# A decoder block with product-key experts: rows of the expert sum moved between POOL and DVE, one engine for a weighting, and one form for all V tiles

## The chip, the core and the metric

One core of a Trainium2 chip. The metric is device time in microseconds (us) of one execution. Engines are named as in the profile: PE (TensorE), DVE (VectorE), ACT (ScalarE), POOL (GpSimd), SP (SyncE, which here only issues DMAs).

## What is computed

A decoder block on 512 tokens of width 1024: three attention branches, merged by gates and added to x, then a sum over experts that are looked up for each token. Only the second part is touched here:

```python
v1, i1 = lax.top_k(s1, 16)                  # per head (8): scores against 128 keys, twice
v2, i2 = lax.top_k(s2, 16)
sv, si = lax.top_k(v1[..., :, None] + v2[..., None, :], 16)
experts = e1 * 128 + e2                     # 128 experts per token out of 16384
act = gelu(h . u[experts]) * softmax(sv)
x = x + sum(act * v[experts])
```

u and v are tables of 16384 rows of 1024 float32 numbers.

## The kernel before

The 512 tokens are four blocks of 128. Blocks 0 and 1 go the sparse way, blocks 2 and 3 the dense way.

**Sparse: rows.** For each of a block's 128 slots, POOL issues an indirect DMA (line 832) that fetches one row of u for each of the 128 tokens, 128 x 1024 numbers; DVE multiplies it by h and sums (line 842), into acts. After 128 such u rows come 128 v rows, which DVE adds to x1 with their weights (line 851, `step`). The 512 rows stand in one list, JOBS, and `step` takes the next. There is a second form for v rows, `apart=True`: ACT scales the row (line 847) and POOL adds it to x1 (line 848). Rows are fetched ahead into buffers, 4 in general, 6 where `ahead` is AHEAD + MORE, so that with the one in use up to seven are under way. All v rows of a block add into the same tile (mg in the profile), one after the other.

**Dense.** For blocks 2 and 3 PE multiplies h by all of u, in 128 tiles of 128 experts (`dense_u`, line 953: 8 float32 matmuls of 256 columns, which the profile records as 16), and ACT's gelu writes the activations (ga, line 955). The gates are spread from the chosen slots over all experts ("spreading", below). Then PE multiplies the 128 activation tiles by all of v (`dense_v`, the V stage).

**The stages at the end, in program order.** (1) The search for blocks 1 to 3: scores on PE, top 16 on DVE (MAX, MATCH_REPLACE, MAX_INDEX), candidates on POOL (line 688). A credit lets one v row of block 0 in for every PER_ROW = 2.8 units of search, in the form on POOL. (2) From here on the order on POOL, DVE and PE is that of the program. PE does 24 u tiles (COVER); DVE does `weigh`, then the choices of blocks 2, 3 and 1 (`choose`, lines 771 to 801: which candidates were chosen, by small integer steps and comparisons in bf16) and turns block 1's into row numbers (`numbers_of`, lines 811 to 815). Then come 12 more v rows (BETWEEN). (3) Spreading: 64 batches of 4 tokens. DVE compares slot numbers with 0..127 (line 1008, tile o), the result is weighted by the gates (three batches of four on ACT, line 1014, the fourth on POOL, line 1011), PE multiplies (line 1026), DVE multiplies the kept part into ga (line 1029), ACT copies the rest out (line 1032). A batch is built three ahead of its use. Each batch brings 0.7 rows (STEPS_N), and 25 u tiles are laid between the matmuls. (4) The V stage, 128 steps k. `operands(k+1)`: a V tile is fetched three ahead; three of four are split, hi on ACT (line 1075, whi) and lo on DVE (line 127, wlo), as are the activations (ah line 1073, al line 1077); from k = 32 on ga is first multiplied by its gates (line 1068). PE then does 12 matmuls (lines 141 to 143). Each fourth tile (k % WHOLE == 3) is taken whole, from a buffer of its own (last), in float32 with 4 matmuls, recorded as 8 (line 1091). The 71 u tiles that remain are spread over the first 118 steps, the rows that remain over the first 123.

DVE, PE, POOL and ACT each take their instructions strictly in order.

Of the kernel before, what the change touches and what calls it, by code (L numbers as in the profile page):

```python
# [12 lines left out]
AF = mybir.ActivationFunctionType  # L13
OP = mybir.AluOpType
# [7 lines left out]
NK = 128  # L22
# [4 lines left out]
DENSE = (2, 3)  # L27
# [2 lines left out]
FIRST_U, COVER, DURING, AFTER = 8, 24, 25, 0  # L30
KEPT = FIRST_U + COVER
SPILT = (128 - KEPT) // 2
BETWEEN, UNWEIGHED, IN_RAW = 12, 14, 0
LAG = FIRST_U + COVER + DURING + AFTER
GA_LATE = 6
URING = 6
# [2 lines left out]
GQ_AT, GQ_PARTS = 1, 4  # L39
RAW_MORE = 5  # L40
STEPS_U = 4
WHOLE, STEPS_N = 4, 0.7
AHD = 3
GSPLIT = 4
GT = 4
# [3 lines left out]
AHEAD, ROWS_IN, MORE = 4, 5, 2  # L49
LATER = 400  # L50
PACE = {"search": 9.0, "choose": 8.0, "rows": 3.5}
EARLY_ROWS, PER_ROW = 176, 2.8


@with_exitstack
def tile_block(ctx: ExitStack, tc: tile.TileContext, t: dict, out: bass.AP):
# [947 lines left out]
    def build_sides(n):  # L1004
        i, _, ts = tokens(n)
        eT = slots[i]
        o = sp.tile([128, 2, GT, NK], F32, tag="o", name="o", bufs=AHD + 1)
        V.tensor_tensor(o, numbers[:, None, None, :].to_broadcast([128, 2, GT, NK]),
                        eT[:, :2, ts, None].to_broadcast([128, 2, GT, NK]), op=OP.is_equal)
        if n % 4 == 3:  # L1010
            G.tensor_tensor(o[:, 0], o[:, 0], eT[:, 2, ts, None].to_broadcast([128, GT, NK]), op=OP.mult)
        else:
            for u in range(GT):
                A.activation(o[:, 0, u], o[:, 0, u], AF.Copy, scale=eT[:, 2, ts.start + u:ts.start + u + 1])
# [35 lines left out]

    def fetch_v(k):
        if k < NK:
            pool, n = (gp[0], 1) if k % WHOLE == WHOLE - 1 else (wp, None)
            tag = "last" if n else "raw"
            raw = pool.tile([128, D if n else WSLOT], F32, tag=tag, name=tag, **({"bufs": n} if n else {}))
            v_raw[k] = raw[:, :D]
            nc.sync.dma_start(v_raw[k], t["peer_v"][k * NK:(k + 1) * NK])

    def operands(k):

        whole = k % WHOLE == WHOLE - 1
        fetch_v(k + VFAR)
        get_gates(k + GK, k % GK - GQ_AT)
        raw, a = v_raw.pop(k), ga(k)
        if k >= KEPT:
            m = gq[k - k % GK][:, :, k % GK]
            g = a.rearrange("p (g t) -> p g t", t=TG)
            V.tensor_mul(g, m, g)  # L1068
        if whole:
            return whole, [raw], a, a  # L1070
        ah = gp[0].tile([128, TD], F32R, tag="ah", name="ah")
        al = gp[0].tile([128, TD], F32R, tag="al", name="al")
        A.copy(ah, a)  # L1073
        hi = wp.tile([128, WSLOT], F32R, tag="whi", name="whi")[:, :D]
        A.copy(hi, raw)  # L1075
        w = [x[:, 0] for x in rest((raw, hi, 1, 1), 0.0)]
        V.tensor_sub(al, a, ah.bitcast(F32))
        return whole, w, ah, al

    def dense_v(k, whole, w, ah, al):  # L1080
        if k == 0:
            tags = ["tp", "tp", "sc", "sc"]
            for i in range(ND):
# [2 lines left out]
        for i in range(ND):  # L1086
            tok = slice(i * 128, i * 128 + 128)
            for hf in range(2):
                d = slice(hf * 512, hf * 512 + 512)
                if whole:  # L1090
                    PE.matmul(acc[i, hf], al[:, tok], w[0][:, d], start=k == 0, stop=k == NK - 1)
# [19 lines left out]
    late.append(lp.tile([128, GA_LATE, TD], F32, name="late"))
# [143 lines left out]
```

## Time and profile before

| | us |
|---|---|
| three runs | 1653.95, 1659.4, 1661.33 |
| median | 1659.4 |
| the profiled execution | 1664.65 |
| its span, first to last instruction | 1662.9 |
| mean granted clock of PE | 0.983 |
| POOL's adds of v rows (line 848) | 34, 81.6 busy |
| POOL's weightings (line 1011) | 16, 27.4 busy |
| split V tiles (casts, line 1075) | 96 |

The span is 1.75 us shorter than the time of its execution. Busy times of matmuls overlap, since matmuls are pipelined; where the length of a group of them matters, it is read from the start of one group to the start of the next. In a row of the timeline, the first number is the start, the second the busy time, both in us; the bracket at the end is idle time before the instruction, with what ended it.

### The profile page before, as it was taken

The numbers are of one execution on the slowest core, as the hardware profiler recorded it, in microseconds if no ns is written. First come the engines' busy times: TensorE is split into PE (matmuls) and PEld (weight loads), VectorE is DVE, ScalarE is ACT, GpSimd is POOL, SyncE is SP. The second block draws the span as 40 slices with busy tenths as digits, with TensorE's granted clock in tenths as the row PEclk, the third lists the DMA queues.
The fourth block names the chain that finished last, engine by engine and source line by source line (L and its number), as shares of the span: only waits on it lengthen the run. The fifth ranks groups of instructions, "written<-read, shape, count | busy, mean of one in ns | idle before, by whom it ended". The sixth has DMA issues, their size and how long they took to land.

```text
span 1662.9 us, 25044 instructions
## 1 busy us (share of the span) xinstructions
PE 1579.9 (95%) x8622; PEld 1359.9 (82%) x8622; DVE 1346.5 (81%) x2599; ACT 700.0 (42%) x1562; POOL 806.9 (49%) x656
## 2 busy tenths in 40 slices
PE   5999999999998989997989999999999999999998
PEld 5999799888987988986878998677777777777775
DVE  5677358898988999998989998677777778778886
ACT  6787347545344434544316664222222222222221
POOL 1100012766565555689944545454554455455542
PEclk9999999999998999999999999999999999999999
DMA  7586744998998899867878999999999999999995
GB/s 291 187 277 220 253 143 144 318 345 306 344 314 301 294 334 349 275 216 274 279 274 298 341 352 354 398 409 378 361 392 400 401 388 402 401 401 398 402 366 214
DMA packets 178479, 531.77 MB, mean 320 GB/s; under 512 B 17584, under 2 KB 46512, under 8 KB 178352
## 3 DMA queue, kind: packets, MB, share of 16 engines
q0 software_dynamic: 73728, 268.47, 43.6%
q1 hardware_dynamic: 100016, 249.11, 41.4%
q10 hardware_dynamic: 4608, 12.58, 2.0%
q8 instruction: 68, 1.11, 0.3%
q14 instruction: 59, 0.48, 0.1%
HBM read 515.42 MB, written 14.68 MB: 319 GB/s over the span
## 4 chain that ended last, share of the span: by engine, by line
PE 36%; issue 20%; DMA 20%; POOL 12%; DVE 9%; ACT 2%; SPq 0%; POOLq 0%; DVEq 0%; ACTq 0%
DMA row<-in_peer_v_dram,eidx 10%; POOL row L832 9%; PE mm L953 8%; DMA row<-in_peer_u_dram,eidx 8%; PE mm L142 5%; PE mm L141 5%; PE mm L143 5%; POOL mg L848 2%; PE mm L294 2%; DVE mg L851 2%; PE sc L1026 2%; PE tp L1026 2%; DVE wlo L127 2%; DVE scr L842 1%; PE sc L493 1%
## 5 line engine op out<-in xcount | busy, mean ns | idle before, releaser
L832 POOL DMA_INDIRECT row<-in_peer_u_dram,eidx x256 | 320.2, 1251 | 254.4 <-DVE scr L842 193.7
L832 POOL DMA_INDIRECT row<-in_peer_v_dram,eidx x256 | 319.5, 1248 | 247.5 <-DVE mg L851 170.4
L127 DVE TENSOR_TENSOR wlo<-raw,whi 128x1024 fp32r<-128x1024 f32 (+1 forms) x243 | 307.3, 1266 | 60.0 <-ACT whi L115 33.0
L842 DVE SCALAR_TENSOR_TENSOR scr<-row,own 128x1024 bf16<-128x1024 f32 x256 | 313.6, 1225 | 43.7 <-DMA row<-in_peer_u_dram,eidx 38.5
L851 DVE SCALAR_TENSOR_TENSOR mg<-row,acts,mg 128x1024 f32<-128x1024 f32 x222 | 284.6, 1282 | 44.1 <-DMA row<-in_peer_v_dram,eidx 39.9
L953 PE MATMUL mm<-h2f,hhi 128*128 128x256 f32 x960 | 223.1, 383 | 3.3 <-ACT ga L955 3.2
L953 PE MATMUL mm<-h2f,hlo 128*128 128x256 f32 x960 | 219.6, 379 | 0.9 <-ACT ga L955 0.9
L953 PEld LDWEIGHTS mm<-h2f,hlo 128*128 128x128 f32 x960 | 179.9, 190 | 33.5 <-issue 8.1
L953 PEld LDWEIGHTS mm<-h2f,hhi 128*128 128x128 f32 x960 | 181.3, 192 | 29.3 <-ACT ga L955 4.5
L115 ACT CAST whi<-raw 128x1024 fp32r<-128x1024 f32 (+1 forms) x148 | 154.9, 1049 | 93.0 <-PE mm L142 45.7
L1075 ACT CAST whi<-raw 128x1024 fp32r<-128x1024 f32 x96 | 100.2, 1045 | 140.6 <-DMA raw<-in_peer_v_dram 136.3
L188 POOL TENSOR_TENSOR rsy<-rsv,mhalf 128x4 f32<-128x4 f32 (+5 forms) x25 | 38.8, 1553 | 221.4 <-DVE rsv L187 127.5
L955 ACT ACTIVATE ga<-mm 128x256 f32<-128x256 f32 x116 | 44.1, 382 | 235.2 <-PE mm L953 225.2
L141 PE MATMUL mm<-hhi,whi 128*128 128x384 f32 x320 | 110.3, 345 | 6.5 <-ACT ga L955 5.3
L142 PE MATMUL mm<-hlo,whi 128*128 128x384 f32 x320 | 110.6, 346 | 0.0
L143 PE MATMUL mm<-hhi,wlo 128*128 128x384 f32 x320 | 109.8, 343 | 0.0
L141 PE MATMUL mm<-whi,hhi 128*128 128x256 f32 (+1 forms) x360 | 104.6, 292 | 3.0 <-DVE g L571 1.9
L142 PE MATMUL mm<-wlo,hhi 128*128 128x256 f32 (+1 forms) x360 | 103.1, 287 | 0.5 <-DVE wlo L127 0.5
L143 PE MATMUL mm<-whi,hlo 128*128 128x256 f32 (+1 forms) x360 | 101.7, 284 | 0.0
L141 PE MATMUL sc<-whi,ah 128*128 128x512 f32 x192 | 90.8, 473 | 3.6 <-ACT ah L1073 2.9
L848 POOL TENSOR_TENSOR mg<-mg,row 128x1024 f32<-128x1024 f32 x34 | 81.6, 2399 | 0.7
L1073 ACT CAST ah<-ga 128x256 fp32r<-128x256 f32 x87 | 34.9, 404 | 107.7 <-DVE ga L1068 69.1
(281 smaller groups left out, 3479.8 us busy)
## 6 DMA issues: line engine op xcount, KB each, us to landing
raw<-in_peer_v_dram SPq DMA_DIRECT2D x96, 512.0 KB
hlo<-in_uT_dram SPq DMA_DIRECT2D x60, 512.0 KB
hhi<-in_uT_dram SPq DMA_DIRECT2D x60, 512.0 KB
raw<-in_w_tr_dram SPq DMA_DIRECT2D x48, 512.0 KB
raw<-in_w_nat_dram SPq DMA_DIRECT2D x40, 512.0 KB
last<-in_peer_v_dram SPq DMA_DIRECT2D x32, 512.0 KB
raw<-in_w_o_dram SPq DMA_DIRECT2D x24, 512.0 KB
gd<-st ACTq DMA_DIRECT2D x32, 384.0 KB
```

What stands on the lines that cost most here:

```text
L115: A.copy(hi[:, :n * w], raw[:, :n * w])
L127: V.tensor_sub(lo, raw, hi.bitcast(F32))
L141: PE.matmul(ps, lh, rh, start=first, stop=False)
L142: PE.matmul(ps, lh, rl, start=False, stop=False)
L143: PE.matmul(ps, ll, rh, start=False, stop=last)
L832: G.indirect_dma_start(out=r, out_offset=None, in_=t["peer_" + tab], in_offset=bass.IndirectOffsetOnAxis(ap=eidx[b][:, j:j + 1], axis=0))
L842: V.scalar_tensor_tensor(scr, r, 1.0, h2n[b], op0=OP.mult, op1=OP.mult, accum_out=acts[b][:, c]))
L848: G.tensor_tensor(x1[b], x1[b], r, op=OP.add)
L851: V.scalar_tensor_tensor(x1[b], r, acts[b][:, c], x1[b], op0=OP.mult, op1=OP.add))
L953: PE.matmul(ps[:, :TD], w[:, dc], h2f[dc], start=dc == 0, stop=dc == KC - 1)
L1026: PE.matmul(ps[:, u], o[:, 1, u], o[:, 0, u], start=True, stop=True)
L1075: A.copy(hi, raw)
```

## The change

**Fewer rows on POOL, rows among the choices.** PER_ROW goes from 2.8 to 4.6. By the order of instructions POOL adds 19 v rows instead of 34. The 12 rows behind the choices go; instead a row is let in for each unit that the choices spend (AMONG = 1.0), which gives 36, on DVE. On POOL, at the end of the search, before (mg is the sum, cand the candidates, row a fetched row):

```order
L848 TENSOR_TENSOR mg_2246<-mg_2246,row 128x1024
L688 TENSOR_TENSOR cand<-v_8832 128x3x8
L688 TENSOR_TENSOR cand<-v_8832 128x3x16
L832 DMA row<-in_peer_v_dram,eidx_176 128x1024
L848 TENSOR_TENSOR mg_2246<-mg_2246,row 128x1024
L832 DMA row<-in_peer_v_dram,eidx_176 128x1024
L848 TENSOR_TENSOR mg_2246<-mg_2246,row 128x1024
```

After, at the same place:

```order
L848 TENSOR_TENSOR mg_2246<-mg_2246,row 128x1024
L688 TENSOR_TENSOR cand<-v_8780 128x3x8
L688 TENSOR_TENSOR cand<-v_8780 128x3x16
L832 DMA row<-in_peer_v_dram,eidx_176 128x1024
L848 TENSOR_TENSOR mg_2246<-mg_2246,row 128x1024
L832 DMA row<-in_peer_v_dram,eidx_176 128x1024 x57
L832 DMA row<-in_peer_u_dram,eidx_178 128x1024 x128
```

Up to here the two are alike; before, 15 more pairs of fetch and add follow (the last two rows shown are the first pair), after it only the fetches of rows that DVE will add.

On DVE, in the first choice, before (rj, rb, hot: steps of the choice):

```order
L784 TENSOR_TENSOR rj<-rj,p_9253 128x128
L785 TENSOR_TENSOR rj<-p_9254,rj 128x128
L789 CAST rb<-ri 128x128
L791 CAST idb<-ids_7514 128x128
L794 TENSOR_TENSOR hot<-rb,iota_k 128x2048
L797 TENSOR_TENSOR hot<-hot,idb 128x2048
L800 TENSOR_TENSOR hot<-hot 128x1024
L800 TENSOR_TENSOR hot<-hot 128x512
L800 TENSOR_TENSOR hot<-hot 128x256
```

After, at the same place:

```order
L784 TENSOR_TENSOR rj<-rj,p_9193 128x128
L785 TENSOR_TENSOR rj<-p_9194,rj 128x128
L851 SCALAR_TENSOR_TENSOR mg_2246<-row,acts_177,mg_2246 128x1024
L789 CAST rb<-ri 128x128
L791 CAST idb<-ids_7514 128x128
L794 TENSOR_TENSOR hot<-rb,iota_k 128x2048
L851 SCALAR_TENSOR_TENSOR mg_2246<-row,acts_177,mg_2246 128x1024
L797 TENSOR_TENSOR hot<-hot,idb 128x2048
L851 SCALAR_TENSOR_TENSOR mg_2246<-row,acts_177,mg_2246 128x1024 x2
L800 TENSOR_TENSOR hot<-hot 128x1024
L800 TENSOR_TENSOR hot<-hot 128x512
L800 TENSOR_TENSOR hot<-hot 128x256
```

Rows (L851) now stand among the choice's steps, one or two at a time.

**Spreading.** All 64 weightings are on ACT. STEPS_N goes from 0.7 to 0.8: 51 rows in place of 44.

**V stage.** No tile is whole; each fourth one still has its own buffer (last) but is split like the others. 230 rows are left for it in place of 246. DVE at the beginning of the V stage, before (wlo and al are the lo halves, scr a u row):

```order
L127 TENSOR_TENSOR wlo<-raw,whi 128x1024
L1077 TENSOR_TENSOR al<-ga,ah 128x256
L842 SCALAR_TENSOR_TENSOR scr,acts_179<-row,own 128x1024 x4
L127 TENSOR_TENSOR wlo<-raw,whi 128x1024
L1077 TENSOR_TENSOR al<-ga,ah 128x256
L842 SCALAR_TENSOR_TENSOR scr,acts_179<-row,own 128x1024 x2
```

After:

```order
L127 TENSOR_TENSOR wlo<-raw,whi 128x1024
L1071 TENSOR_TENSOR al<-ga,ah 128x256
L842 SCALAR_TENSOR_TENSOR scr,acts_179<-row,own 128x1024 x2
L127 TENSOR_TENSOR wlo<-last,whi 128x1024
L1071 TENSOR_TENSOR al<-ga,ah 128x256
L842 SCALAR_TENSOR_TENSOR scr,acts_179<-row,own 128x1024 x2
```

The tile from the buffer last, which DVE did not touch before, now has its own wlo and al, and fewer rows stand between two tiles.

The diff, without the lines that only drop the flag `whole`:

```diff
-BETWEEN, UNWEIGHED, IN_RAW = 12, 14, 0
+AMONG, UNWEIGHED = 1.0, 14
-WHOLE, STEPS_N = 4, 0.7
+SPARE, STEPS_N = 4, 0.8
-EARLY_ROWS, PER_ROW = 176, 2.8
+EARLY_ROWS, PER_ROW = 176, 4.6
...
-        if n % 4 == 3:
-            G.tensor_tensor(o[:, 0], o[:, 0], eT[:, 2, ts, None].to_broadcast([128, GT, NK]), op=OP.mult)
-        else:
-            for u in range(GT):
-                A.activation(o[:, 0, u], o[:, 0, u], AF.Copy, scale=eT[:, 2, ts.start + u:ts.start + u + 1])
+        for u in range(GT):
+            A.activation(o[:, 0, u], o[:, 0, u], AF.Copy, scale=eT[:, 2, ts.start + u:ts.start + u + 1])
...
-        if whole:
-            return whole, [raw], a, a
...
-                if whole:
-                    PE.matmul(acc[i, hf], al[:, tok], w[0][:, d], start=k == 0, stop=k == NK - 1)
-                else:
-                    mm3(acc[i, hf], (ah[:, tok], al[:, tok]), (w[0][:, d], w[1][:, d]), k == 0, k == NK - 1)
+                mm3(acc[i, hf], (ah[:, tok], al[:, tok]), (w[0][:, d], w[1][:, d]), k == 0, k == NK - 1)
...
-    for lb in (1, 2):
-        list(choose(cp, f, lb, iota_k, chosen[DENSE[lb - 1]]))
-    list(numbers_of(cp, f, 0, 1, iota_k))
+    ahead[0] = AHEAD + MORE
+    credit[0] = 0.0
+    for job in (*(choose(cp, f, lb, iota_k, chosen[DENSE[lb - 1]]) for lb in (1, 2)), numbers_of(cp, f, 0, 1, iota_k)):
+        for cost in job:
+            credit[0] += cost
+            while credit[0] >= AMONG and done[0] < known[0]:
+                credit[0] -= AMONG
+                step()
     known[0] = len(JOBS)
-    ahead[0] = AHEAD + MORE
-    for _ in range(BETWEEN):
-        step()
```

More of the change, by code (lines that the diff above doesn't have):

```diff
@@ L1052, in fetch_v @@
         if k < NK:
-            pool, n = (gp[0], 1) if k % WHOLE == WHOLE - 1 else (wp, None)
+            pool, n = (gp[0], 1) if k % SPARE == SPARE - 1 else (wp, None)
             tag = "last" if n else "raw"
@@ L1059, in operands @@
     def operands(k):
-        whole = k % WHOLE == WHOLE - 1
         fetch_v(k + VFAR)
@@ L1077, in operands, with dense_v @@
         V.tensor_sub(al, a, ah.bitcast(F32))
-        return whole, w, ah, al
-    def dense_v(k, whole, w, ah, al):
+        return w, ah, al
+    def dense_v(k, w, ah, al):
         if k == 0:
```

## The prediction

> **What bounds the kernel now.** I read the page first, then busy time by stage, then the timeline of each engine where one stage meets the next.
>
> ```profile
> PE 1579.9 (95%) x8622; PEld 1359.9 (82%) x8622; DVE 1346.5 (81%) x2599; ACT 700.0 (42%) x1562; POOL 806.9 (49%) x656
> ```
>
> The shares are averages, so I cut the end of the run into its stages. Columns: stretch, length, then busy us (instructions) of PE, weight loads, DVE, ACT, POOL, the granted clock, the DMA share and GB/s.
>
> ```profile
> 774.30:820.40 46.10, 42.00 (x181) 34.74 (x179) 42.91 (x37) 21.38 (x30) 42.60 (x25) 0.96 0.82 274
> 820.40:865.60 45.20, 45.17 (x210) 39.75 (x211) 42.68 (x65) 4.86 (x13) 20.99 (x15) 1.00 0.72 249
> 865.60:876.00 10.40, 0.47 (x4) 0.26 (x3) 6.97 (x6) 1.46 (x5) 6.55 (x5) 0.73 1.03 416
> 876.00:1022.50 146.50, 146.50 (x917) 135.70 (x918) 137.94 (x180) 101.46 (x345) 70.16 (x59) 0.98 0.92 332
> 1022.50:1622.50 600.00, 594.98 (x2437) 460.16 (x2436) 457.42 (x625) 149.35 (x253) 307.12 (x236) 1.00 1.02 391
> 1622.50:1662.90 40.40, 32.52 (x109) 20.86 (x107) 26.29 (x34) 7.68 (x11) 8.30 (x6) 0.95 0.58 212
> ```
>
> The first two rows are the three choices on DVE, with the 24 covering u tiles on PE. The third is a hole: PE does 0.47 us in 10.4. The fourth is the spreading, where PE never stops and DVE nearly never. The fifth is the V stage while u tiles last: PE 595 of 600 us, so it is PE that sets its length, with DVE at 76% and the DMA engines full. The sixth is its tail, which no single engine fills. The chain that ended last shows the hole again:
>
> ```profile
> 865.92 9.93 issue
> 875.85 2.05 PE sc L1026 x8
> ```
>
> PE has ended the covering tiles at 865.9 and starts the spreading at 875.85, since the one-hot sides it needs come late from DVE. DVE's timeline, and POOL's adds of rows, tell why:
>
> ```profile
> 779.30 2.90 DVE L771 TENSOR_SCALAR sh<-pos 128x128 uint32<-128x128 uint32 x1
> 817.37 3.12 DVE L773 TENSOR_SCALAR sh<-pos 128x128 uint32<-128x128 uint32 x1
> 840.12 0.22 DVE L771 TENSOR_SCALAR sh<-pos 128x128 uint32<-128x128 uint32 x1
> 840.63 0.23 DVE L773 TENSOR_SCALAR sh<-pos 128x128 uint32<-128x128 uint32 x1
> 852.31 0.29 DVE L811 SCALAR_TENSOR_TENSOR e<-e,e 128x128 f32<-128x128 f32 x1
> 853.97 10.52 DVE L851 SCALAR_TENSOR_TENSOR mg<-row,acts,mg 128x1024 f32<-128x1024 f32 x8
> 874.10 4.61 DVE L1008 TENSOR_TENSOR o<-tg,eT 128x1024 f32<-128x1024 f32 x4
> ```
>
> ```profile
> 772.45 2.36 POOL L848 TENSOR_TENSOR mg<-mg,row 128x1024 f32<-128x1024 f32 x1
> 776.07 2.38 POOL L848 TENSOR_TENSOR mg<-mg,row 128x1024 f32<-128x1024 f32 x1
> 829.03 2.35 POOL L848 TENSOR_TENSOR mg<-mg,row 128x1024 f32<-128x1024 f32 x1
> ```
>
> The same small shift takes 0.23 us alone and 3.12 us while POOL adds a row: DVE stands still for the add. The third choice runs undisturbed, 840.12 to 852.31: 12.2 us. Three of them and the last three steps of the numbers (852.31 to 853.97) make 38.2 us; they took 74.7 (779.30 to 853.97). So POOL's late adds cost DVE 36 us, and the 12 rows behind them 20 us more (853.97 to 874.10).
>
> **Part 1: fewer rows to POOL, rows among the choices.** By the order POOL keeps 19 of its 34 adds, 36 rows stand among the choices in place of 12 behind them. The nineteenth add is the one at 772.45 (829.03 is the last, 15 follow the nineteenth), over at 774.8, before the choices begin at 779.3. So the 36 us of stalls go. What comes in is 24 more rows on DVE, and a row's price stands in the spreading, in three batches of DVE's timeline:
>
> ```profile
> 926.51 1.28 DVE L851 SCALAR_TENSOR_TENSOR mg<-row,acts,mg 128x1024 f32<-128x1024 f32 x1
> 927.70 0.28 DVE L1029 TENSOR_TENSOR ga<-tp,ga 128x128 f32<-128x128 f32 x1
> 930.22 0.28 DVE L1029 TENSOR_TENSOR ga<-sc,ga 128x128 f32<-128x128 f32 x1
> 931.56 0.28 DVE L1029 TENSOR_TENSOR ga<-tp,ga 128x128 f32<-128x128 f32 x1
> ```
>
> A row between other work costs 1.19 us (926.51 to 927.70), one behind another 1.32 (the 10.52 / 8 above); the order has mostly singles, so 1.25: 36 x 1.25 = 45 us. DVE would end at 779.3 + 38.2 + 45 = 862.5, against 874.1, and PE could start 1.75 us later, as now (874.10 to 875.85): 864.3. Is PE there? Its cover:
>
> ```profile
> 781.48 8.86 PE L953 MATMUL mm<-h2f,hhi 128*128 128x256 f32 x32 [2.74 <-ACT ga L955]
> 834.35 10.52 PE L953 MATMUL mm<-h2f,hlo 128*128 128x256 f32 x48
> 844.71 10.52 PE L953 MATMUL mm<-h2f,hhi 128*128 128x256 f32 x48
> 775.12 3.62 PE L953 MATMUL mm<-h2f,hhi 128*128 128x256 f32 x16
> ```
>
> Three u tiles take 10.36 us (834.35 to 844.71), one 3.45, 24 from 775.12 on 82.9; with the 2.74 us wait kept and 0.3 for transposes PE ends at 861. So the hole closes to about 3 us and the spreading starts 11.6 us earlier. The rows must come in time: POOL issues them, with nothing else to do, and up to seven are under way. Of today's twelve the last four came late; the first and the last of these, with the wait in brackets:
>
> ```profile
> 866.55 1.28 DVE L851 SCALAR_TENSOR_TENSOR mg<-row,acts,mg 128x1024 f32<-128x1024 f32 x1 [2.05 <-issue]
> 872.90 1.28 DVE L851 SCALAR_TENSOR_TENSOR mg<-row,acts,mg 128x1024 f32<-128x1024 f32 x1 [0.45 <-DMA row<-in_peer_v_dram,eidx]
> ```
>
> These waits are 0.45 to 2.05 us, behind eight rows taken back to back. The new ones stand 2.3 us apart (82 us for 36), so I charge 2.6 us in all. Behind a DVE that waits for a row stands the rest of the choices, and PE waits for that. **Term: -9 us** (0 to -11.6).
>
> **Part 2: spreading, 51 rows in place of 44, all weighting on ACT.** By the rows L1029 above a batch with a row takes DVE 2.52 us (927.70 to 930.22), one without 1.34. Seven rows more are 8.3 us: 137.9 + 8.3 = 146.2 of today's 146.5. PE was full, so nothing is gained; DVE is now as full as PE, and its 8.6 us of waits can't all be used. Between 0 (all used) and +8.3 (none) I take **+3.5 us**. ACT gets 16 x 4 more weightings:
>
> ```profile
> L1014 ACT ACTIVATE o<-o,eT 128x128 f32<-128x128 f32 x191 | 60.8, 390 | 17.0 <-DVE o L1008 13.7 <-issue 3.3
> ```
>
> 64 x 60.8/191 = 20.4 us, so 122 busy of 146.5. Three batches of lead cover that; if not, rival D. On POOL the weightings stood ahead of the rows' issues; without them rows come no later, for which I take nothing.
>
> **Part 3: every V tile split.** 16 rows leave the V stage (246 to 230), and 32 whole tiles become split ones.
>
> ```profile
> 1404.10 1.88 PE L1091 MATMUL sc<-last,ga 128*128 128x512 f32 x4
> 1407.53 3.62 PE L953 MATMUL mm<-h2f,hlo 128*128 128x256 f32 x16
> 1410.80 0.58 PE L141 MATMUL sc<-whi,ah 128*128 128x512 f32 x1
> 1413.76 0.39 PE L141 MATMUL sc<-whi,ah 128*128 128x512 f32 x1
> 1416.51 3.62 PE L953 MATMUL mm<-h2f,hlo 128*128 128x256 f32 x16
> ```
>
> Their busy times overlap, so I read from start to start. A whole tile: 1404.10 to 1407.53, 3.43 us. A split one: 1413.76 to 1416.51, 2.75 us, or 2.96 behind a u tile, which is then itself 3.27 in place of 3.45. Either way a split tile saves about 0.66 us of PE. The Trainium skill, "FP8 and Floating Point Precision", TensorE Precision Notes, says that true FP32 makes four passes through the array; three reduced passes would then be 3/4 of 3.43, 0.86 us saved, and this term an estimated 25 us where the rows give 19. While u tiles last (118 of 128 tiles, 29 of them whole) that is 29 x 0.66 = 19 us. In the tail PE isn't the bound, and I take nothing. The cover of this term is DVE:
>
> ```profile
> L851 DVE SCALAR_TENSOR_TENSOR mg<-row,acts,mg 128x1024 f32<-128x1024 f32 x119 | 152.7, 1283 | 33.6 <-DMA row<-in_peer_v_dram,eidx 32.3
> L842 DVE SCALAR_TENSOR_TENSOR scr<-row,own 128x1024 bf16<-128x1024 f32 x118 | 144.3, 1223 | 26.1 <-DMA row<-in_peer_u_dram,eidx 22.0 <-issue 1.3 <-DVE scr L842 0.9
> L127 DVE TENSOR_TENSOR wlo<-raw,whi 128x1024 fp32r<-128x1024 f32 x90 | 111.0, 1234 | 26.4 <-ACT whi L1075 20.6 <-issue 3.9 <-ACT ga L955 1.9
> L1077 DVE TENSOR_TENSOR al<-ga,ah 128x256 fp32r<-128x256 f32 x81 | 34.0, 420 | 48.4 <-ACT ah L1073 47.7 <-ACT whi L1075 0.6
> ```
>
> Each split tile adds a 1.234 us and a 0.420 us subtraction: 29 x 1.654 = 48 us; 16 rows at 1.25 take away 20. DVE goes from 457 to 485 us of a stage of 581: 84% for 76%. ACT, at 149 of 600, has room for two more casts a tile. On SP the buffer of every fourth tile comes free when DVE has split it, no longer when PE is done with it, so its load is issued no later. The DMA engines are full too, but 16 rows of 0.524 MB (128 x 1024 x 4 bytes) are 8.4 MB less, at 391 GB/s 21 us: were they the bound, the gain would be the same. With some waits on the fuller DVE: **-17.5 us** (-21 to -9, rival A's end).
>
> **Sum.** -9 + 3.5 - 17.5 = -23 us on the profiled execution's 1664.65: 1641.65. That execution lies 5.25 above the median of the runs shown, 1659.4; on that scale 1636.4.
>
> **The rivals.** *A, DVE paces the V stage.* Its idle time in rows L127 and L1077 (75 us) is waiting for ACT's halves, which may come with every tile: with 32/24 of it, 485 + 100 = 585, more or less, and with some of the row waits 591. The stage gains 9 us, the sum is -14.5: 1644.9. *B, the same with nothing given up:* if all 142.6 us of idle time (600 - 457.4) stay, the stage takes 628, and the sum is +22.5: 1681.9. Against B: 60 us of that idle time are rows that DVE came too early for, and a later DVE doesn't wait for them. *C, slower: the rows among the choices come late.* The place is POOL's issue:
>
> ```profile
> L832 POOL DMA_INDIRECT row<-in_peer_v_dram,eidx x256: 935/993/3086, 562.1 to 1632.1; - x128
> ```
>
> An issue takes 0.99 us in the middle and 3.09 at worst (min/median/max). If each of the 36 takes the worst and 0.3 between, DVE ends at 780.6 + 36 x 3.39 = 903, the spreading starts 28.5 us late, and the sum is +14.5: 1673.9. It decides from 3.0 us a row on, where the start is 14 us late and the sum is nothing; below 2.3 it costs nothing. The median speaks against it. The Trainium skill, "SBUF — State Buffer", SBUF: two separate sides, says that POOL can't write a DMA's descriptors while certain DVE operations hold the shared port; by that rule C's stretched issues would be the common case among the choices, but the median above says that they are rare in the whole run. *D, ACT paces the spreading:* should all its 45 us of waits stay beside 122 of work, the stage takes 167, 20.4 more, and the sum is -6.1: 1653.3.
>
> **How the numbers follow.** The forecast gets 0.57, A 0.17, B 0.06, C 0.10, D 0.10. A measurement of this kernel can tell about 0.5%, 8.3 us, from no change. Forecast and A are faster; D and a third of C's way lie within; B and the rest of C are slower: 0.74, 0.13, 0.13. The low end takes every best bound: -11.6 + 0 - 21 = -32.6, 1626.8, and 2 us for the scatter of the runs: 1625. The high end takes in D and C up to where the sum is nothing, and 2.6 for the scatter: 1662. Left out are about 0.13 above and 0.05 below.
>
> **What would show it.** Right: no DVE shift over 1 us behind the search; spreading starting near 865 with a hole of PE under 5 us; 148 to 152 us of spreading; the V stage with PE still near 99% and some 582 us to the last u tile. Wrong: rows among the choices with waits that sum to over 15 us (C), PE waiting for wlo or al in the V stage (A, B), ACT full and PE waiting for it in the spreading (D).

## The result and the profile after

The kernel after takes 1633.94 us (median of 4 runs, 1632.55 to 1638.87) against 1660.37 for the kernel before on the same chip (4 runs): the ratio is 0.9853, with a 95% interval from 0.9819 to 0.9888. A ratio is always the time of the kernel named over that of the kernel before, with its 95% interval in brackets. A second measurement with the experiments gave 0.9846 (0.982 to 0.9872). The profiled execution of after took 1635.28 us (span 1633.5), 29.4 less than that of before (1664.65, span 1662.9). Busy time and the shares of the chain that ended last, on the page of after:

```profile
PE 1559.2 (95%) x8750; PEld 1384.0 (85%) x8750; DVE 1368.6 (84%) x2678; ACT 743.4 (46%) x1675; POOL 788.7 (48%) x625
PE 68%; DMA 11%; DVE 7%; issue 7%; POOL 3%; ACT 2%; SPq 0%; DVEq 0%; POOLq 0%; ACTq 0%
```

PE stood for 36% of that chain before; POOL fell from 12% to 3% and "issue" from 20% to 7%. For a comparison by stage both traces are cut at the same events: the first u tile of the cover, the first matmul of the spreading, the end of the spreading, the last u tile, the end. Busy time by stage (columns as in the prediction), of before and then of after:

```profile
775.10:875.85 100.75, 86.68 (x388) 73.87 (x387) 91.62 (x107) 27.54 (x46) 69.61 (x44) 0.96 0.80 277
875.85:1022.50 146.65, 146.65 (x917) 135.85 (x918) 138.09 (x180) 101.61 (x345) 70.16 (x59) 0.98 0.92 332
1022.50:1619.40 596.90, 591.88 (x2423) 457.60 (x2422) 454.35 (x622) 148.03 (x251) 305.13 (x235) 1.00 1.02 392
1619.40:1662.90 43.50, 35.62 (x122) 23.43 (x120) 29.35 (x37) 9.00 (x13) 10.29 (x8) 0.95 0.59 217
```

```profile
779.80:865.50 85.70, 83.37 (x388) 73.17 (x387) 78.24 (x116) 10.55 (x28) 51.96 (x38) 1.00 0.98 376
865.50:1010.05 144.55, 144.53 (x918) 134.14 (x918) 143.07 (x203) 115.71 (x408) 48.50 (x48) 1.00 0.94 353
1010.05:1591.70 581.65, 574.09 (x2540) 479.11 (x2539) 476.22 (x648) 190.17 (x311) 321.67 (x219) 1.00 1.02 388
1591.70:1633.50 41.80, 33.58 (x134) 24.30 (x132) 33.84 (x43) 11.83 (x18) 11.09 (x8) 0.99 0.62 225
```

The spreading starts 10.3 us earlier (865.5 for 875.85), takes 2.1 us less, the V stage to its last u tile 15.2 us less, the tail 1.7 us less: 29.3 in all. At the first seam, where the choices give way to the spreading, DVE is no longer held up by POOL's adds, and PE decides. From DVE's and PE's timelines of after (L1008 builds the one-hot sides, L851 is a row, L1023 the spreading's matmul):

```profile
777.31 0.23 DVE L773 TENSOR_SCALAR sh<-pos 128x128 uint32<-128x128 uint32 x1
855.27 2.59 DVE L851 SCALAR_TENSOR_TENSOR mg<-row,acts,mg 128x1024 f32<-128x1024 f32 x2
863.76 4.62 DVE L1008 TENSOR_TENSOR o<-tg,eT 128x1024 f32<-128x1024 f32 x4 [5.90 <-ACT eT L997]
```

```profile
773.30 6.66 PE L953 MATMUL mm<-h2f,raw 128*128 128x256 f32 x16 [4.63 <-DMA raw<-in_uT_dram]
862.68 0.38 PE L995 MATMUL acc<-cst,e 128*128 128x128 f32 x2
865.52 1.32 PE L1023 MATMUL sc<-o 128*128 128x128 f32 x8 [2.35 <-issue]
```

The shift takes 0.23 us. DVE ends choices and 36 rows at 857.9 and waits 5.9 us for eT, which ACT copies after PE's transposes at 862.7. PE's cover began late: 4.63 us of waiting for the load of the eighth u tile, which then took 6.66 us in place of 3.62. That wait differs between profiled executions, so the start of the spreading lies between 857.8 and 865.5 in the eight executions below that share the part ahead of it with the kernel after, and between 870.6 and 875.9 in the three that share it with the kernel before. Numbers behind the start are therefore read as stage lengths.

### The profile page after: what moved, and what is told of

Its sections match the earlier page's. It is cut to its first block, busy times and chain, and to the rows that moved or that the text cites. A ratio compares the mean times of both kernels' runs of the same rounds, so it can differ in the third digit from the quotient of the medians.

```text
span 1633.5 us, 25556 instructions
## 1 busy us (share of the span) xinstructions
PE 1559.2 (95%) x8750; PEld 1384.0 (85%) x8750; DVE 1368.6 (84%) x2678; ACT 743.4 (46%) x1675; POOL 788.7 (48%) x625
## 3 DMA queue, kind: packets, MB, share of 16 engines
q1 hardware_dynamic: 100016, 249.11, 41.8%
## 4 chain that ended last, share of the span: by engine, by line
PE 68%; DMA 11%; DVE 7%; issue 7%; POOL 3%; ACT 2%; SPq 0%; DVEq 0%; POOLq 0%; ACTq 0%
PE mm L953 24%; PE mm L142 5%; PE mm L141 5%; PE mm L143 5%; DMA row<-in_peer_u_dram,eidx 4%; PE sc L142 3%; PE sc L143 3%; PE sc L141 3%; PE tp L141 3%; PE tp L143 3%; PE tp L142 3%; DMA raw<-in_peer_v_dram 3%; DMA row<-in_peer_v_dram,eidx 2%; POOL row L832 2%; PE mm L294 2%
## 5 line engine op out<-in xcount | busy, mean ns | idle before, releaser
L832 POOL DMA_INDIRECT row<-in_peer_v_dram,eidx x256 | 351.7, 1374 | 278.9 <-DVE mg L851 152.4
L832 POOL DMA_INDIRECT row<-in_peer_u_dram,eidx x256 | 333.2, 1301 | 280.4 <-DVE scr L842 165.9
L851 DVE SCALAR_TENSOR_TENSOR mg<-row,acts,mg 128x1024 f32<-128x1024 f32 x237 | 303.4, 1280 | 5.2 <-DMA row<-in_peer_v_dram,eidx 2.3
L953 PE MATMUL mm<-h2f,hhi 128*128 128x256 f32 x960 | 219.3, 379 | 0.0
L188 POOL TENSOR_TENSOR rsy<-rsv,mhalf 128x4 f32<-128x4 f32 (+5 forms) x25 | 38.8, 1553 | 220.0 <-DVE rsv L187 126.8
L141 PE MATMUL sc<-whi,ah 128*128 128x512 f32 x256 | 115.0, 449 | 10.3 <-ACT ah L1067 7.4
L1071 DVE TENSOR_TENSOR al<-ga,ah 128x256 fp32r<-128x256 f32 x116 | 48.9, 421 | 73.2 <-ACT ah L1067 69.7
L142 PE MATMUL sc<-wlo,ah 128*128 128x512 f32 x256 | 101.6, 397 | 1.5 <-DVE wlo L127 0.8
```

The costliest lines, as they stand in the source:

```text
L141: PE.matmul(ps, lh, rh, start=first, stop=False)
L142: PE.matmul(ps, lh, rl, start=False, stop=False)
L832: G.indirect_dma_start(out=r, out_offset=None, in_=t["peer_" + tab], in_offset=bass.IndirectOffsetOnAxis(ap=eidx[b][:, j:j + 1], axis=0))
L851: V.scalar_tensor_tensor(x1[b], r, acts[b][:, c], x1[b], op0=OP.mult, op1=OP.add))
L953: PE.matmul(ps[:, :TD], w[:, dc], h2f[dc], start=dc == 0, stop=dc == KC - 1)
```

## The experiments

Stages of all profiled executions, cut as above (us), and the median times. Below the first two rows, each group of four kernels ran on one chip; there the kernel before took 1659.45, 1659.39 and 1661.77. "V + tail" runs from the end of the spreading to the end.

| kernel | spreading starts | spreading | V stage | tail | V + tail | time |
|---|---|---|---|---|---|---|
| before | 875.9 | 146.7 | 596.9 | 43.5 | 640.4 | 1660.4 |
| after | 865.5 | 144.5 | 581.7 | 41.8 | 623.5 | 1633.9 |
| v_split_only | 870.6 | 146.5 | 596.3 | 41.8 | 638.1 | 1656.2 |
| no_v_split | 859.3 | 146.2 | 596.9 | 38.8 | 635.7 | 1647.6 |
| fewer_pool_rows_only | 863.1 | 144.5 | 624.2 | 45.1 | 669.3 | 1673.5 |
| rows_behind | 881.8 | 146.5 | 582.5 | 43.3 | 625.8 | 1656.0 |
| half_tiles | 874.9 | 147.3 | 588.3 | 43.5 | 631.8 | 1653.8 |
| pool_weighs | 857.8 | 144.5 | 584.8 | 41.8 | 626.6 | 1637.1 |
| rows_done_sooner | 862.4 | 144.5 | 594.8 | 34.9 | 629.7 | 1640.8 |
| even_tail | 864.2 | 144.5 | 614.1 | 18.3 | 632.4 | 1642.9 |
| after_again | 861.5 | 144.5 | 587.1 | 42.0 | 629.1 | 1635.4 |
| more_bytes | 865.4 | 144.5 | 592.0 | 44.4 | 636.4 | 1649.0 |
| more_dve | 863.2 | 146.2 | 589.1 | 46.2 | 635.3 | 1647.7 |
| early_u | 870.3 | 144.5 | 585.5 | 40.6 | 626.1 | 1642.8 |

Five of these executions have the V stage of after unchanged: after, after_again, rows_behind, pool_weighs and early_u. Their V stages took 581.7 to 587.1 us (584.8 in the middle) and V + tail 623.5 to 629.1 (626.1 in the middle). A difference of less than 5 us between single profiles of this stage shows nothing by itself.

### v_split_only: the split alone

Before, with the V tiles of after (the main lines of the edit):

```
-        if whole:
-            return whole, [raw], a, a
...
-                if whole:
-                    PE.matmul(acc[i, hf], al[:, tok], w[0][:, d], start=k == 0, stop=k == NK - 1)
-                else:
-                    mm3(acc[i, hf], (ah[:, tok], al[:, tok]), (w[0][:, d], w[1][:, d]), k == 0, k == NK - 1)
+                mm3(acc[i, hf], (ah[:, tok], al[:, tok]), (w[0][:, d], w[1][:, d]), k == 0, k == NK - 1)
```

> The kernel before, with every V tile split and nothing else changed: rows, POOL's share of them and POOL's weighting stay as they were. Theory 1, TensorE paces the V stage: 29 tiles save 0.66 us each, 19 us, less what new waits take, as in the kernel after, where the stage lost 15.2 us; start of spreading (875.85 in the trace of before) and spreading (146.7 us) do not move; the time is 13 to 17 us below the kernel before. Theory 2, the transfers pace it and the gain after came from the rows that no longer load there: as many bytes move in the stage, so it stays at 597 us and the time within 3 us of before. Theory 3, VectorE paces it: 25 more rows than in the kernel after, 31 us at 1.25 us, fill its 584 us from 479 to 510 us busy, and a gain of at most 8 us is left.

Ratio 0.9984 (0.997 to 0.9999): some 3 us, and the V stage is as before (596.3 for 596.9). PE's work did shrink, by 13.3 us (591.9 to 578.6) and not by the 19 that were reckoned, and waits took its place. The stage's busy times, then PE's and ACT's groups in it (behind the second bar the idle time before them):

```profile
1017.10:1613.40 596.30, 578.57 (x2539) 480.20 (x2538) 494.17 (x680) 190.47 (x316) 333.21 (x235) 0.99 1.02 392
L141 PE MATMUL sc<-whi,ah 128*128 128x512 f32 x234 | 106.6, 455 | 16.9 <-ACT ah L1070 16.9
L1072 ACT CAST whi<-raw 128x1024 fp32r<-128x1024 f32 x89 | 93.2, 1047 | 146.5 <-DMA raw<-in_peer_v_dram 88.8 <-PE tp L143 53.1 <-DMA gd<-st 3.7
L1072 ACT CAST whi<-last 128x1024 fp32r<-128x1024 f32 x30 | 31.4, 1046 | 63.2 <-DMA last<-in_peer_v_dram 50.3 <-PE tp L143 12.9
```

PE waits 16.9 us for ah, where in the kernel before it waited 1.1. ACT's timeline in this stage tells why: ah stands in its queue behind the cast of a V tile whose load hasn't landed.

```profile
1396.36 1.04 ACT L1072 CAST whi<-raw 128x1024 fp32r<-128x1024 f32 x1 [7.57 <-DMA raw<-in_peer_v_dram]
1397.31 0.38 ACT L955 ACTIVATE ga<-mm 128x256 f32<-128x256 f32 x1
1397.59 0.39 ACT L1070 CAST ah<-ga 128x256 fp32r<-128x256 f32 x1
```

```profile
1398.03 0.79 PE L141 MATMUL sc<-whi,ah 128*128 128x512 f32 x1 [2.75 <-ACT ah L1070]
1397.21:1404.04 6.83, 6.01 (x14) 4.76 (x15) 5.96 (x8) 2.70 (x6) 3.03 (x2) 0.50 0.96 359
```

The second row is the stretch behind this wait, in the columns of the stages: PE's granted clock was 0.50 there, so beside the 2.75 us of the wait PE lost half its pace for 6.8 us. The wait for late loads sums to 139 us on ACT (88.8 + 50.3). Theory 1 fails; the stage's length is the one that theory 2 gives, at 392 GB/s. Theory 3 had DVE busy for 510 us; it was busy for 494. Whether it is the bytes is the question of half_tiles and more_bytes.

### no_v_split: all but the split

After, with every fourth tile whole:

```
-SPARE, STEPS_N = 4, 0.8
+WHOLE, STEPS_N = 4, 0.8
...
+        if whole:
+            return whole, [raw], a, a
...
+                if whole:
+                    PE.matmul(acc[i, hf], al[:, tok], w[0][:, d], start=k == 0, stop=k == NK - 1)
```

> The kernel after with the V stage of before: every fourth tile whole; rows among the choices, ten rows fewer for POOL and weighting on ACT stay. Theory 1, TensorE paces the V stage: start of spreading at 865 and spreading in 145 us as after, the V stage back at 595 to 598 us, so 10 to 13 us below the kernel before and 14 to 17 us above the kernel after. Theory 2, transfers pace it: the rows that load before the stage take their 21 us with them whatever the tiles are, so about 25 us below the kernel before, as the kernel after.

Ratio 0.9924 (0.9898 to 0.995), 11.8 us below before. The V stage is at 596.9 again, now with PE full, fewer bytes, and ACT waiting 63 us for loads instead of the 129.4 of before:

```profile
1005.50:1602.40 596.90, 590.77 (x2424) 458.55 (x2423) 435.76 (x591) 147.46 (x252) 299.69 (x220) 1.00 1.01 380
L1072 ACT CAST whi<-raw 128x1024 fp32r<-128x1024 f32 x89 | 92.8, 1044 | 69.5 <-DMA raw<-in_peer_v_dram 63.3 <-PE tp L143 5.9 <-ACT ah L1070 0.2
```

Theory 1 holds here: with whole tiles, PE decides. So the V stage of before stands under two limits of about the same height: PE's work with whole tiles (590.8 to 591.9 us busy, 5 to 6 us of waits), and what 235 rows with their loads allow, 596 us. Either half of the change leaves the stage at 596 to 597; only both together lower it, to 581.7 to 587.1. The medians, which don't hang on single profiles, say the same: -3.3 and -11.8 make -15.1, and the whole change is -26.4.

### fewer_pool_rows_only: PER_ROW alone

```
-EARLY_ROWS, PER_ROW = 176, 2.8
+EARLY_ROWS, PER_ROW = 176, 4.6
```

> The kernel before with POOL given ten rows fewer during the search, and nothing else: the twelve rows stay behind the choices, the ten rows go to later stages. Theory 1, POOL's adds stretched VectorE's small instructions in the choices: the adds end before the choices, VectorE is done with choices and twelve rows early, and spreading starts at 865 to 867 when the transposes of TensorE's u tiles are ready, 9 to 11 us sooner; the ten rows cost nothing in a V stage that TensorE paces; the time is 9 to 13 us below before. Theory 2, it is the rows' place that made the start sooner and not POOL's count: the start stays within 2 us of 875.85 and the time within 3 us of before. Theory 3, the ten rows are paid in the V stage, by their transfers (5.2 MB, 13 us at 391 GB/s): the start is sooner and the time within 3 us of before.

Ratio 1.0085 (1.0064 to 1.0105): slower. (POOL's adds went from 34 to 19, fifteen and not the ten of the expectation.) At the seam theory 1 holds, with 12.8 us for its 9 to 11. DVE's timeline:

```profile
776.73 0.23 DVE L773 TENSOR_SCALAR sh<-pos 128x128 uint32<-128x128 uint32 x1
788.80 0.23 DVE L773 TENSOR_SCALAR sh<-pos 128x128 uint32<-128x128 uint32 x1
800.87 0.23 DVE L773 TENSOR_SCALAR sh<-pos 128x128 uint32<-128x128 uint32 x1
814.20 6.56 DVE L851 SCALAR_TENSOR_TENSOR mg<-row,acts,mg 128x1024 f32<-128x1024 f32 x5
861.30 4.62 DVE L1008 TENSOR_TENSOR o<-tg,eT 128x1024 f32<-128x1024 f32 x4 [22.77 <-ACT eT L997]
```

There is a choice every 12.07 us, the last step is done at 814.2, and after twelve rows DVE stands idle for 22.8 us until PE's cover ends: the spreading starts 12.8 us earlier than before. But fifteen rows are left over, and the V stage pays for them, more than theory 3 had it:

```profile
1007.60:1631.80 624.20, 598.57 (x2424) 459.95 (x2423) 469.86 (x644) 147.36 (x250) 327.64 (x249) 0.99 1.01 387
L141 PE MATMUL sc<-whi,ah 128*128 128x512 f32 x176 | 83.0, 472 | 20.6 <-ACT ah L1073 19.5 <-ACT whi L1075 1.1
```

248 rows instead of 235 up to the last u tile cost 27.3 us, 2.1 us a row, where their bytes at 387 GB/s are 1.35 us (0.524 MB). Of the remaining 10 us, 6.7 may be PE's: for the same matmuls it is busy 598.6 us where it was 591.9, at a granted clock of 0.99 for 1.00, and it waits 19.5 us for ah. That these parts add up in this way isn't shown. DVE is idle here for 154 of 624 us.

### rows_behind: the same 36 rows in one block

```
-AMONG, UNWEIGHED = 1.0, 14
+BETWEEN, UNWEIGHED = 36, 14
...
-            while credit[0] >= AMONG and done[0] < known[0]:
-                credit[0] -= AMONG
-                step()
...
+    for lb in (1, 2):
+        list(choose(cp, f, lb, iota_k, chosen[DENSE[lb - 1]]))
+    list(numbers_of(cp, f, 0, 1, iota_k))
+    for _ in range(BETWEEN):
+        step()
```

> The kernel after with its 36 rows in one block behind the two choices and the numbering, instead of among them. Theory 1, the place among the small instructions matters, since back to back a row waits for the issue of its gather on POOL: the 36 rows take some 1.55 us each in place of 1.27 us, VectorE ends some 10 us later than 857.8, at 868, and spreading starts 3 to 6 us later than in the kernel after; the time is 3 to 6 us above it. Theory 2, the order does not matter because TensorE's u tiles end at 862.7 in both: the time is within 2 us of the kernel after (some 26 us below before).

Ratio 0.998 (0.9964 to 0.9995): the place of the rows is worth some 22 us. Theory 1 is right that the rows come late, but its size is four times too small. DVE's timeline: the first five rows of the block, the first that came late, the last nine, and the first work of the spreading:

```profile
814.48 6.56 DVE L851 SCALAR_TENSOR_TENSOR mg<-row,acts,mg 128x1024 f32<-128x1024 f32 x5
821.83 1.28 DVE L851 SCALAR_TENSOR_TENSOR mg<-row,acts,mg 128x1024 f32<-128x1024 f32 x1 [0.79 <-DMA row<-in_peer_v_dram,eidx]
868.27 11.85 DVE L851 SCALAR_TENSOR_TENSOR mg<-row,acts,mg 128x1024 f32<-128x1024 f32 x9 [0.29 <-DMA row<-in_peer_v_dram,eidx]
880.04 4.61 DVE L1008 TENSOR_TENSOR o<-tg,eT 128x1024 f32<-128x1024 f32 x4
```

From 821.83 to 868.27 a row comes every 2.1 us and waits for its gather; DVE is done at 880.0, and PE stands still for 20.7 us. What sets this pace shows in the last two columns of the stretch of the choices and of the stretch of the late rows:

```profile
776.00:814.00 38.00, 38.00 (x175) 33.38 (x174) 36.19 (x90) 4.38 (x12) 0.00 (x0) 0.99 0.45 148
821.00:868.30 47.30, 40.12 (x188) 35.08 (x186) 28.32 (x24) 5.08 (x13) 27.97 (x26) 0.97 1.02 404
```

During the choices POOL issues nothing (by the program's order, because the buffers hold rows that DVE hasn't taken yet), and the DMA engines have a share of 0.45. Behind the choices they are full, at 404 GB/s, while POOL's issues take 28.0 of 47.3 us. A row of 0.524 MB every 2.1 us and a u tile of the same size every 3.45 us make 402 GB/s, so it is the transfers that set the pace here, and not POOL's issues as theory 1 had it. Among the choices 36 rows take 81 us, 2.25 us each, with the DMA engines at 0.98 and 376 GB/s (first row of after by stage, above): that is about the pace at which they can come, and DVE hardly waits (0.4 us for all 36). In the V stage this kernel is as after (582.5 us).

### half_tiles: 8.4 MB less, all rows kept

v_split_only, and every fourth V tile loaded by half (the lines that split such a tile read the loaded half twice; they are left out here):

```
+            part = D // 2 if k % 4 == 1 else D
+            nc.sync.dma_start(v_raw[k][:, :part], t["peer_v"][k * NK:(k + 1) * NK, :part])
```

> The kernel before with every V tile split, as in v_split_only, but of every fourth V tile only the first half of the columns is loaded, and both halves of the split are taken from it (so the output isn't the reference's). That is 32 x 0.262 MB = 8.4 MB less to transfer in the V stage, as much as 16 rows are, with every row, every issue on POOL and every instruction on VectorE, ACT and TensorE kept. Theory 1, the transfers hold the V stage of v_split_only at 596 us (233.7 MB at 392 GB/s): with 225.3 MB they need 575 us, TensorE's 582 us as in the kernel after decide, and the time is 12 to 16 us below v_split_only, so 15 to 19 us below the kernel before. Theory 2, it is the rows' instructions on VectorE or their issues on POOL that hold it: the stage stays at 594 to 598 us and the time within 2 us of v_split_only, 1 to 5 us below before.

Ratio 0.9967 (0.9952 to 0.9982). The V stage lost 8.0 us against v_split_only, of the 14 that theory 1 gave it. The median time lost only 2.4 us, and the intervals of the two ratios overlap; in the profiled executions this spreading started 4.3 us later:

```profile
1022.20:1610.50 588.30, 575.54 (x2539) 476.97 (x2538) 492.75 (x678) 190.05 (x313) 334.46 (x234) 1.00 1.01 384
```

ACT's waits for loads fell from 139 to 106 us, against 67 in the kernel after (50.1 + 17.0). With the bytes of after, but the DVE work of v_split_only, the stage lies between the two kernels, 1 us above the highest of the five unchanged V stages. That points to the bytes as a part of the cost and not the whole; the next two kernels show each part better.

### more_bytes and more_dve: the two costs of 16 rows, one at a time

After, with one addition each in the V stage, first that of more_bytes, then that of more_dve; after_again is the kernel after on the same chip:

```
+        if k % 2 == 1:
+            beside_ = gp[0].tile([128, D // 4], F32, tag="beside", name="beside", bufs=1)
+            nc.sync.dma_start(beside_, t["peer_v"][k * NK:(k + 1) * NK, :D // 4])
```

```
+        if k % 8 == 3:
+            scr = big.tile([128, D], BF16, tag="junk", name="scr")
+            V.scalar_tensor_tensor(scr, h2n[1], 1.0, h2n[1], op0=OP.mult, op1=OP.mult)
```

> The kernel after, unchanged, on the same chip as the next three kernels, to measure them by. Expected: 1632 to 1640 us, start of spreading between 858 and 866 as upstream scatter has it, spreading 144.5 us, 581 to 585 us to the last u tile.

> The kernel after with 64 further loads of 128 x 256 numbers in the V stage, into a buffer that nothing reads: 8.4 MB more to transfer, as much as 16 rows, and nothing more on VectorE or POOL. Theory 1, transfers at their limit make V tiles late: the stage of 582 us grows by 6 to 12 us, ACT's casts wait longer for the loads than the 67 us after, and the time is 6 to 12 us above the kernel after. Theory 2, it was the 16 rows' work on VectorE: within 2 us of the kernel after.

> The kernel after with 16 further products of 128 x 1024 on VectorE in the V stage, whose results nothing reads: 20 us more of VectorE, as much as 16 rows take, with no transfer. Theory 1, transfers: VectorE goes from 476 to 496 of 582 us and the time stays within 2 us of the kernel after. Theory 2, VectorE paces the V tiles that have no u tile between them: the stage grows by 6 us or more and so does the time.

after_again: 1635.4 us, as expected, except that its V stage took 587.1 us, 5.4 more than in the first profile: so much do executions of one kernel differ there. more_bytes: 0.993 (0.9905 to 0.9956), 13.5 us above after_again. more_dve: 0.9914 (0.9888 to 0.994), 12.3 us above. By both theories 1 only more_bytes would be slower, by both theories 2 only more_dve; both kernels are. V stage of after_again, more_bytes and more_dve, with ACT's casts of V tiles from the common buffers and, of the first and the last, of the activations:

```profile
1006.00:1593.10 587.10, 575.80 (x2539) 479.80 (x2538) 476.56 (x648) 190.32 (x311) 321.55 (x219) 0.99 1.01 385
L1069 ACT CAST whi<-raw 128x1024 fp32r<-128x1024 f32 x89 | 93.2, 1048 | 116.9 <-DMA raw<-in_peer_v_dram 60.6 <-PE tp L143 56.0 <-ACT ah L1067 0.2
L1067 ACT CAST ah<-ga 128x256 fp32r<-128x256 f32 x107 | 43.1, 404 | 82.5 <-PE tp L142 50.0 <-DVE ga L1064 29.5 <-issue 2.7
```

```profile
1009.90:1601.90 592.00, 576.82 (x2539) 478.10 (x2539) 475.78 (x648) 190.14 (x311) 325.01 (x219) 1.00 1.03 394
L1072 ACT CAST whi<-raw 128x1024 fp32r<-128x1024 f32 x89 | 93.2, 1047 | 118.4 <-DMA raw<-in_peer_v_dram 78.3 <-PE tp L143 38.5 <-issue 1.2
```

```profile
1009.40:1598.50 589.10, 577.04 (x2541) 478.74 (x2540) 492.86 (x663) 191.23 (x311) 319.90 (x219) 1.00 1.01 384
L1069 ACT CAST whi<-raw 128x1024 fp32r<-128x1024 f32 x89 | 93.1, 1046 | 106.3 <-PE tp L143 54.7 <-DMA raw<-in_peer_v_dram 51.1 <-ACT ah L1067 0.2
L1067 ACT CAST ah<-ga 128x256 fp32r<-128x256 f32 x107 | 43.1, 404 | 101.4 <-DVE ga L1064 48.8 <-PE tp L142 48.4 <-issue 2.7
```

More bytes lengthen the wait for loads to 78.3 us, at 394 GB/s; in the five unchanged V stages it was 48.5 to 60.6. More DVE leaves it there (51.1) and lengthens ACT's wait for DVE's product ga to 48.8 us, for 26.3 to 31.4 in the five; half_tiles, with 16 rows more on DVE and no more bytes than after, shows the same (45.0). The addition of more_dve made DVE busy for 16.3 us more, not 20. V + tail grows by 7 and 6 us against after_again, by 13 and 12 us against the first profile of after.

The times of the profiled executions differ by more (11.2 and 9.6 us), but 3.9 and 3.4 of that arose ahead of the V stage, which these edits don't touch. The two prices don't seem to add: against the middle of the five they are 10 and 9 us, while 16 rows, which cost both at once and 16 issues on POOL besides, are worth 12 (v_split_only; 9 to 15 against single profiles). What the issues cost was not tried by itself.

Why DVE matters when it is busy for only 84% of the stage (more_dve) shows where a V tile has no u tile ahead of it, as in the tail of after; DVE's timeline:

```profile
1603.47 0.42 DVE L1064 TENSOR_TENSOR ga<-gq,ga 128x256 f32<-128x256 f32 x1
1605.28 2.60 DVE L851 SCALAR_TENSOR_TENSOR mg<-row,acts,mg 128x1024 f32<-128x1024 f32 x2
1607.80 0.42 DVE L1064 TENSOR_TENSOR ga<-gq,ga 128x256 f32<-128x256 f32 x1
```

With two rows a V tile takes DVE 4.33 us (1603.47 to 1607.80) and PE 2.75 to 2.96, and the program prepares one tile ahead. That this also makes the waits within the stage is an inference from these rows; it was not tried by itself.

### pool_weighs: weighting back on POOL

After, with every fourth batch weighted by G.tensor_tensor again (lines 1010 to 1011 of before).

> The kernel after with every fourth batch of the spreading weighted on POOL again, as before. Theory 1, TensorE paces the spreading: 16 additions of work on POOL, 27 us, stretch VectorE's 143 us by some 3.5 us, to 146.6 beside TensorE's 144.5, and the time is 0 to 3 us above the kernel after. Theory 2, ACT's share holds the spreading back, as rival D had it: the stage gets shorter and the time 2 us or more below the kernel after. Theory 3, the weightings on POOL delay the issues of the 51 rows behind them: the spreading takes 150 us or more, and the time is over 5 us above.

Ratio 0.9874 (0.9851 to 0.9897), that of after within its interval; the spreading took 144.5 us as after. PE paces it either way, as theory 1 has it, and ACT's part of the change is worth nothing that shows. The stretch of DVE that theory 1 reckoned with did not come: DVE was busy for 142.8 us, for 143.1 in after.

### rows_done_sooner and even_tail: the rows' end

The edit of rows_done_sooner; even_tail has NK - 8 in this place, and NK - 4 for NK - 10 in the line that sets the u tiles:

```
-        while done[0] < min(len(JOBS), start + (len(JOBS) - start) * (k + 1) // (NK - 5)):
+        while done[0] < min(len(JOBS), start + (len(JOBS) - start) * (k + 1) // (NK - 12)):
```

> The kernel after, with the last row due at V tile 116 in place of 123. Theory 1, in the tail VectorE sets the pace: with two rows a tile it works 4.33 us a tile where TensorE needs 2.8, so without rows the last tiles take 2.8 us each and the tail 32 to 35 us for 41.8; but the rows' transfers move into a V stage that is 6 us short of the transfers' bound (225.7 MB at 392 GB/s are 576 of 582 us): 9 rows more there are 4.7 MB, and the stage grows by up to 6 us. In sum 2 to 5 us below the kernel after. Theory 2, the tail is set by the end of the loads, not by VectorE: no change within 2 us.

> The kernel after, with the last row due at V tile 120 in place of 123 and the last u tile at 124 in place of 118, so that TensorE's work reaches as far as the rows do. Theory 1: bytes a V tile stay as they are, TensorE keeps 4.94 us of work a tile for 5.04, the rows end before the u tiles, and the V stage with its tail costs TensorE's 608 us and some 8 us of waits, 616 for 623: 5 to 8 us below the kernel after. Theory 2, the tail is set by the loads or by the output at the end: within 2 us of it.

0.9899 (0.9872 to 0.9927) and 0.9904 (0.9886 to 0.9921): neither is faster than after. rows_done_sooner by stage:

```profile
1006.90:1601.70 594.80, 578.98 (x2541) 480.15 (x2539) 491.67 (x661) 190.81 (x311) 319.86 (x226) 0.99 1.01 389
1601.70:1636.60 34.90, 30.90 (x134) 24.75 (x132) 19.25 (x30) 11.65 (x18) 0.00 (x0) 0.99 0.33 113
```

The tail shrank by 6.9 us, as DVE's pace there has it, and the stage ahead of it grew by 8 to 13 for eleven more rows. V + tail came to 629.7, no less than in the five unchanged ones (623.5 to 629.1). even_tail ended no better (632.4). A row moved into the stage costs about what it saved in the tail.

### early_u: the eighth u tile's load

```
+            w = u_raw.pop(k) if k in u_raw else load_raw(t["uT"][k], D)[:, :D]
+            if k + 1 < FIRST_U:
+                u_raw[k + 1] = load_raw(t["uT"][k + 1], D)[:, :D]
```

> The kernel after with each of the first eight u tiles loaded one u tile earlier. In the trace of after TensorE waits 4.63 us for the load of the eighth and then takes 6.66 us for it where it takes 3.62 otherwise. Theory 1: this wait and the slow stretch go, TensorE's cover ends earlier, and the spreading starts 4 to 6 us sooner, until VectorE, which ends the choices at 857.8, decides; the time is 4 to 6 us below the kernel after. Theory 2, the buffer that is held longer delays the loads of the search: no gain within 2 us.

Ratio 0.9885 (0.9856 to 0.9915), 7 us above after_again: a miss for theory 1. The loads stand earlier in the program, but the last one was issued no earlier: 0.5 us ahead of the start of PE's sixth and seventh u tiles (765.46), as in after (761.12 and 761.60). What holds it stays open. SP's queue, and PE with the wait for the landing:

```profile
764.99 0.33 SPq L109 DMA_DIRECT2D raw<-in_uT_dram  x1
778.46 6.24 PE L955 MATMUL mm<-h2f,raw 128*128 128x256 f32 x16 [5.92 <-DMA raw<-in_uT_dram]
```

None of these kernels beats after.

## Why the prediction was right, and where it was not

The forecast for the profiled execution was -23 us; it measured -29.4, and -26.4 between the medians. Of the 6.4 us that were missed, 5.6 lie in the spreading; the misses of the other terms nearly cancel.

**Start of spreading, -9, measured -10.3.** Right, with its mechanism: POOL's late adds were the stalls. The undisturbed choices take 12.07 us each, 12.2 by the forecast, and fewer adds alone moved the start by 12.8 us. Two pieces of the sum were off: the 2.6 us charged for late rows weren't needed, and DVE, done at 857.9 and not at 862.5, isn't last any more; PE's cover is. (Of these 4.6 us, 2.5 come from the choices' start, at 776.8 and not at 779.3.) That the term fits to 1.3 us is partly luck, since the starts differ by 5 and 8 us among the executions that share this part; by the middle of the three and of the eight, 874.9 and 862.8, it is -12.1. Rival C asked for 3.0 us a row; among the choices rows came every 2.25 us. POOL's issues there took

```profile
L832 POOL DMA_INDIRECT row<-in_peer_v_dram,eidx x38: 936/1164/2032, 779.7 to 856.8; - x38
```

1.16 us in the middle against 0.95 behind the choices in rows_behind, far from C. The Trainium skill, "SBUF — State Buffer", SBUF: two separate sides, has POOL unable to write descriptors while some DVE operations hold the shared port. That could stand behind these 0.2 us in the median, but no run here shows it. What the forecast didn't see is what the place of the rows is worth: 22 us, by rows_behind.

**Spreading, +3.5, measured -2.1.** The step that failed: "DVE is now as full as PE, and its 8.6 us of waits can't all be used". Nearly all were used: DVE is busy 143.1 of 144.5 us and PE never waited. DVE's work was also 3 us less than the 146.2 reckoned. So the seven rows cost nothing, where 3.5 us were charged. The 2 us gained besides go with PE's clock behind the hole. The first five microseconds of the spreading, in before, after and no_v_split:

```profile
875.85:880.85 5.00, 5.00 (x18) 4.46 (x19) 5.00 (x6) 4.41 (x16) 1.86 (x2) 0.52 0.50 198
```

```profile
865.50:870.50 5.00, 4.98 (x30) 4.67 (x31) 5.00 (x6) 5.00 (x19) 0.00 (x0) 1.00 0.18 75
```

```profile
859.26:864.26 5.00, 5.00 (x22) 4.46 (x23) 5.00 (x6) 5.00 (x19) 0.00 (x0) 0.66 0.61 247
```

Behind 9.93 us without work PE ran 18 matmuls at a granted clock of 0.52, behind 2.35 us 30 at 1.00. It isn't the length of the hole alone: no_v_split and more_dve, with a hole of 2.35 us too, had 0.66 there and took 146.2 us. The rows don't decide it: fewer_pool_rows_only, with the spreading of before and a hole of 2.35 us, took 144.5. So this gain comes with the shorter hole and is luck as far as the sum goes, which didn't contain it; two of the ten executions with such a hole (2.35 to 2.67 us) missed most of it. What decides it then isn't shown. Rival D fell: ACT was busy 115.7 us and PE waited for none of it.

**V stage, -17.5, measured -15.2, and -9.8 to -15.2 by the five profiles of this V stage.** The size came out, a little high, because both halves of the change were made. PE's share was nearly right: busy 591.9 to 574.1 us, 17.8 for 29 tiles, 0.61 a tile for the 0.66 read from the trace. By the Trainium skill, "FP8 and Floating Point Precision", TensorE Precision Notes, true FP32 makes four passes; three in their place would save an estimated 0.86 us a tile. The trace agrees only in the direction, with 0.61. The step that failed is "it is PE that sets its length". PE set it together with the rows, at about the same height, and the sentence on the DMA engines, "were they the bound, the gain would be the same", treats as alternatives what had to happen together: each alone gives nothing that shows (596.3 and 596.9 us for 596.9). Of rival A something is true: 16.3 us more on DVE cost 6 to 12 us. Idle time of an engine (18% of DVE's here) was taken for free room; that it is missing tile by tile is the inference made above.

**Tail, 0, measured -1.7.** Within what profiles of one kernel differ by.

The signs to watch for in the prediction came true for the seam (0.23 us shifts, start at 865.5, a hole of 2.35) and for the stage (581.65 us for some 582, PE busy for 98.7% of it); the 148 to 152 us of spreading did not.

## What to carry to other kernels

When a stage shows one engine at 99% and the transfers at their ceiling too, take the price of each away on paper separately: a change that relieves only one may give nothing, and two that are worth nothing each can be worth 10 to 15 us together. Work with a transfer in it is cheapest where its transfers have time to come, among other instructions of its engine rather than in a block behind them: there the transfers stood still first and were the limit afterwards. And where one engine feeds another with little buffering between them, the idle time of the feeding one isn't free room: 16 us more on an engine busy for 82% of a stage cost 6 to 12.

## What the runs showed of the hardware

Over the whole V stage the kernels moved 380 to 394 GB/s with the DMA engines' share at 1.00 to 1.03; rows_behind moved 404 in the 47 us behind its choices. PE's granted clock over the first 5 us behind a hole was 0.52 after 9.93 us without work; after 2.35 us it was 1.00 in the kernel after and 0.66 in no_v_split and more_dve. Beside a POOL add of 128 x 1024 (2.37 us) a DVE shift of 128 x 128 took up to 3.12 us; where the adds ended before the choices, the same shift took 0.23 in each of them.
